# A down projection in seven block products: four groups of feature pairs with sums on the chip, or one group of nine pairs with the inputs' sums made a stage earlier

## The chip, the cores and the metric

The kernel runs on one core of a Trainium2 chip. The engines of a core work side by side, each on its own list of instructions in order: TensorE (PE, matrix products), VectorE (DVE), ScalarE (ACT), GpSimd (POOL) and SyncE (SP, which here issues nearly all DMAs). The metric is the device time of one execution in microseconds (us).

## The reference, cut to what matters

One layer of a hybrid decoder (three kinds of token mixer, then a gated feed-forward part) on 1024 tokens of width 1024. The change lies in the feed-forward part and its last product:

```
fn = rmsnorm(h, ffn_norm_g)
h  = h + (silu(fn @ w_gate) * (fn @ w_up)) @ w_down      # w_gate, w_up: 1024 x 2816, w_down: 2816 x 1024
return rmsnorm(h, final_norm_g)
```

The hidden values `silu(..) * (..)` are 2816 features by 1024 tokens, all in float32.

## The kernel before, in words

**Precision.** Every operand of a product is split into a high part (a rounded copy, ACT, the `act.copy` of `split`) and a low part (operand minus high part, a subtraction on DVE or POOL). A product takes three matmuls: high x high, low x high, high x low.

**Features, pairs, blocks.** The 2816 features are 22 tiles of 128. Two tiles are a pair, so there are 11 pairs (`NP`), p = 0 to 10. Gate and up projection go pair by pair (class `GateUp`, one object a pair, "the gate stage"). A pair's weights and inputs are cut into 2 x 2 blocks, and instead of eight block products seven are made, from sums and differences of blocks (Strassen's scheme in Winograd's form). The products are numbered 1 to 7, and their order in the gate stage is 1, 2, 6, 5, then 7 and 3, then 4. The block outputs of a pair, `out(q, ...)` with q = 0 to 3, are a feature tile and a half of the tokens each; `out` makes sigmoid (ACT) and two multiplications (DVE, L1303 and L1304) into the tile `gs`, and SP stores it to `s_hid` in DRAM (L1305). q = 0 comes after product 2, then q = 3, 1 and 2.

**The down projection** starts when the gate stage ends. It takes the features as pairs too, in 2 x 2 blocks: the left operand is `w_down` (two feature tiles by two output halves, `a11` to `a22`), the right one the hidden values (two feature tiles by two token halves, `b11` to `b22`). Pairs are taken in groups of 2, 2, 2 and 3 (`down_group`). In a group each of the seven products is accumulated in four PSUM banks over the pairs of the group (12 matmuls of 128x512 a pair), in the order 1, 6, 2, 5, 7, 3, 4 on three sets of four banks: A (products 1, 2), B (6, 5, 3), C (7, 4). After product 1 its four banks are copied to `E1` (ACT, L1508) or added to it; after each of the other products DVE adds four banks to the residual in `hF0` to `hF7` (`gather`, L1084). What a product needs is made from whole tiles that SP loaded once (`next_raw`, 512 KB each): sums in place on DVE (`sub` L1081, `add` L1084), and the split of the left and of the right operand, each 128x512, their low parts mostly on POOL (L1078). After the last group `E1` is added to the twelve places that share product 1, on POOL. Features 2304 to 2815 (four tiles) go last, as plain products beside the final norm (`last`, `down`, `last_part`; L1560 to L1562).

**The order.** The source is written product by product, but a scheduler with a model of times of its own lays out each engine's instructions; an engine then runs its list in order, and a wait holds up all that stands behind it.

Of the kernel before, what the change touches and what calls it, by code (L numbers as in the profile page):

```python
# [11 lines left out]
F32 = mybir.dt.float32  # L12
# [20 lines left out]
KV_LORA = 256  # L33
D_FF = 2816
NF = D_FF // 128
EPS = 1e-6
NEG = -1e30

# [20 lines left out]
def tile_hybrid_block(ctx: ExitStack, tc: tile.TileContext, a: dict):  # L59
# [23 lines left out]
    s_hid = dram.tile([NF, 128, SEQ], F32, name="s_hid")  # L83
# [992 lines left out]
    def split(hi, lo, value, eng):  # L1076
        act.copy(hi, value)  # L1077
        eng.tensor_tensor(lo, value, f32(hi), op=ALU.subtract)  # L1078

    def sub(out, x, y):  # L1080
        dve.tensor_tensor(out, x, y, op=ALU.subtract)  # L1081

    def add(out, x, y, eng=None):
        (eng or dve).tensor_tensor(out, x, y, op=ALU.add)  # L1084
# [16 lines left out]
    def q_tile(name):  # L1101
        return tq.tile([128, 512], F32, tag="q", name=name)
# [38 lines left out]
    def operand():  # L1141
        t = hid_tile("op")
        return t[:, HALF[0]], t[:, HALF[1]]
# [92 lines left out]
    class GateUp:  # L1236


        def __init__(self, p):
            self.p = p  # L1240
            self.before = {}
            self.w, self.raw = [], []

        def load_early(self):
# [54 lines left out]
        def out(self, q, gate, up):  # L1299

            h, s = (f1_tile(f1a, "gs", 1), f1_tile(f1a, "sig", 1)) if q == 0 else (q_tile("gs"), q_tile("sig"))
            act.activation(s, gate, AF.Sigmoid)
            dve.tensor_tensor(h, gate, s, op=ALU.mult)  # L1303
            dve.tensor_tensor(h, h, up, op=ALU.mult)  # L1304
# [131 lines left out]
    f2 = ctx.enter_context(tc.tile_pool(name="f2", bufs=1, reuse_waits="tile"))  # L1436
    nraw = nop = 0

    def next_raw(src):
        nonlocal nraw  # L1440
        pl = fr if nraw % 16 < 8 else f2
        nraw += 1
        return raw_tile(pl, src)

    def operand():
        nonlocal nop
        t = fo.tile([128, 1024], F32R, tag="op", bufs=4, name="op") if nop % 16 >= 12 else hid_tile("op")
        nop += 1
        return t[:, HALF[0]], t[:, HALF[1]]
# [5 lines left out]
    LO_DVE = (1, 6, 2)  # L1455

    def down_group(p0, n):
        W, H = [], []
        for e in range(n):
            w, h = ([next_raw(src[2 * (p0 + e) + i]) for i in range(2)] for src in (a["w_down"], s_hid))  # L1460
            W.append((w[0][:, HALF[0]], w[1][:, HALF[0]], w[0][:, HALF[1]], w[1][:, HALF[1]], q_tile("tt")))
            H.append((h[0][:, HALF[0]], h[0][:, HALF[1]], h[1][:, HALF[0]], h[1][:, HALF[1]], q_tile("tt")))

        def operands(i):
            out = []
            for (a11, a12, a21, a22, tw), (b11, b12, b21, b22, th) in zip(W, H):
                if i == 6:
                    sub(a21, a11, a21)
                    sub(b12, b22, b12)
                    sub(tw, a22, a21)  # L1470
                    add(th, b12, b11)
                elif i == 5:
                    add(a11, tw, a11)
                    sub(b11, b22, th)
                elif i == 3:
                    sub(a12, a12, tw)
                elif i == 4:
                    sub(th, b21, th)
                left = {1: a11, 6: tw, 2: a12, 5: a11, 7: a21, 3: a12, 4: a22}[i]
                right = {1: b11, 6: th, 2: b21, 5: b11, 7: b12, 3: b22, 4: th}[i]  # L1480
                if p0 == 0 and i == 1:
                    hl = [wa.tile([128, 1024], F32R, tag=f"w{x}", name=f"w{x}") for x in ("hi", "lo")]
                    pair = [[t[:, s] for t in hl] for s in HALF]
                else:
                    pair = [operand(), operand()]
                split(*pair[0], left, pool)
                split(*pair[1], right, dve if i in LO_DVE else pool)
                out.append(pair)
            return out

        def product(i, banks, start):
            for e, ((wh, wl), (hh, hl)) in enumerate(operands(i)):
                for o in range(4):
                    os = slice(128 * o, 128 * (o + 1))
                    first, last = start and e == 0, e == n - 1
                    pe.matmul(banks[o], wh[:, os], hh, start=first, stop=False, skip_group_check=not start)  # L1496
                    pe.matmul(banks[o], wl[:, os], hh, start=False, stop=False, skip_group_check=not start)  # L1497
                    pe.matmul(banks[o], wh[:, os], hl, start=False, stop=last, skip_group_check=not start)  # L1498

        lo, hi = HALF  # L1500
        A = banks4()
        product(1, A, True)
        if p0 == 0:
            for k in range(KT):
                sp.dma_start(hT[k], s_h[k])
        for o in range(4):
            if p0 == 0:
                act.copy(E1[o], A[o])  # L1508
            else:
                add(E1[o], E1[o], A[o])  # L1510
        B = banks4()
        product(6, B, True)
        gather(B, 4, lo)
        product(2, A, False)
        gather(A, 0, lo)
        product(5, B, False)
        gather(B, 4, hi)
        C = banks4()
        product(7, C, True)
        gather(C, 4, hi)  # L1520
        product(3, B, False)
        gather(B, 0, hi)
        product(4, C, False)
        gather(C, 4, lo)

    p0 = 0
    for n in (2, 2, 2, 3):
        down_group(p0, n)
        p0 += n
# [7 lines left out]
    for e, f in enumerate(range(2 * p0, NF)):  # L1537
        w, h = next_raw(a["w_down"][f]), next_raw(s_hid[f])
        if e < 2:
            hl = [wa.tile([128, 1024], F32R, tag=f"w{x}", name=f"w{x}") for x in ("hi", "lo")]  # L1540
            split(*hl, w, pool)
            W = [[t[:, s] for t in hl] for s in HALF]
        else:
            W = [operand() for _ in HALF]
            for x, s in zip(W, HALF):
                split(*x, w[:, s], pool)
        H = [operand() for _ in HALF]
        for x, s in zip(H, HALF):
            split(*x, h[:, s], dve)
        last.append((W, H))  # L1550

    def down(o, t0, n):
        ts = slice(t0, t0 + n)
# [166 lines left out]
```

## Time and profile before

| | us |
|---|---|
| median of 3 runs (1813.46 to 1816.01) | 1813.62 |
| the profiled execution | 1819.26 |
| its span in the trace | 1817.3 |
| first matmul of the down projection, from the span's start | 1555.0 |
| first matmul of the four plain tiles | 1755.4 |

The times in the trace's rows count from the start of the span. A row of an instruction has its start, its duration, its engine, the source line, and in brackets the idle time of the engine before it and who ended that. A line such as L1084 is that of a helper and is shared by many calls, so the tile's name tells them apart: `hF` with a bank is a gather, `u` and `r` are the gate stage's, `raw` and `tt` are sums of operands.

### The profile page before, as it was taken

The numbers are of one execution on the slowest core, as the hardware profiler recorded it, in microseconds if no ns is written. First come the engines' busy times: TensorE is split into PE (matmuls) and PEld (weight loads), VectorE is DVE, ScalarE is ACT, GpSimd is POOL, SyncE is SP. The second block draws the span as 40 slices with busy tenths as digits, with TensorE's granted clock in tenths as the row PEclk, the third lists the DMA queues.
The fourth block names the chain that finished last, engine by engine and source line by source line (L and its number), as shares of the span: only waits on it lengthen the run. The fifth ranks groups of instructions, "written<-read, shape, count | busy, mean of one in ns | idle before, by whom it ended". The sixth has DMA issues, their size and how long they took to land.

```text
span 1817.3 us, 26447 instructions
## 1 busy us (share of the span) xinstructions
PE 1722.8 (95%) x9769; PEld 1506.0 (83%) x9769; DVE 1214.3 (67%) x1801; ACT 860.0 (47%) x1878; POOL 858.4 (47%) x597
## 2 busy tenths in 40 slices
PE   7969999999999999999999998999999999799997
PEld 7859998999987778998888876778888888677787
DVE  8686655777544673455576558967776667899854
ACT  7545564555566646775544424422232223334333
POOL 4433334343366557563321345634333234678783
PEclk9969999999998999999999998999999999899999
DMA  4211232222443546347221342232222233733102
GB/s 157 60 53 44 78 88 73 64 70 66 116 148 106 187 159 171 103 124 263 78 88 53 108 140 102 64 99 83 80 76 81 71 98 140 286 100 95 47 1 93
DMA packets 121012, 186.93 MB, mean 103 GB/s; under 512 B 21986, under 2 KB 81412, under 8 KB 120884
## 3 DMA queue, kind: packets, MB, share of 16 engines
q1 hardware_dynamic: 101488, 169.69, 29.6%
q10 hardware_dynamic: 19396, 15.56, 2.8%
q8 instruction: 77, 1.26, 0.3%
q14 instruction: 51, 0.42, 0.1%
HBM read 131.61 MB, written 53.60 MB: 102 GB/s over the span
## 4 chain that ended last, share of the span: by engine, by line
PE 68%; DVE 17%; ACT 4%; issue 3%; DMA 3%; POOL 3%; SPq 1%; ACTq 0%; DVEq 0%; POOLq 0%
PE d_ps L142 8%; PE d_ps L143 8%; PE d_ps L144 8%; PE b_ps L1295 7%; PE b_ps L1297 7%; PE b_ps L1296 7%; DVE raw L1081 2%; PE ptg L317 2%; PE b_ps L1498 1%; PE b_ps L1497 1%; PE ptg L319 1%; PE pv L295 1%; PE b_ps L1496 1%; PE pv L296 1%; DVE hF L1084 1%
## 5 line engine op out<-in xcount | busy, mean ns | idle before, releaser
L142 PE MATMUL d_ps<-hnh,whi 128*128 128x384 f32 (+6 forms) x744 | 247.3, 333 | 1.4 <-DVE go L534 0.7
L144 PE MATMUL d_ps<-hnl,whi 128*128 128x384 f32 (+6 forms) x744 | 246.7, 332 | 0.0
L143 PE MATMUL d_ps<-hnh,wlo 128*128 128x384 f32 (+6 forms) x744 | 245.6, 330 | 0.0
L131 POOL TENSOR_TENSOR wlo<-wraw,whi 128x1024 fp32r<-128x1024 f32 (+1 forms) x57 | 135.9, 2385 | 212.0 <-ACT whi L129 203.1
L1078 POOL TENSOR_TENSOR op<-raw,op 128x512 fp32r<-128x512 f32 x83 | 125.2, 1534 | 42.1 <-ACT op L1077 38.9
L142 PEld LDWEIGHTS d_ps<-hnh,whi 128*128 128x128 f32 (+1 forms) x744 | 140.4, 189 | 5.5 <-DVE go L534 1.3
L144 PEld LDWEIGHTS d_ps<-hnl,whi 128*128 128x128 f32 (+1 forms) x744 | 140.6, 189 | 3.3 <-issue 1.0
L143 PEld LDWEIGHTS d_ps<-hnh,wlo 128*128 128x128 f32 (+1 forms) x744 | 140.4, 189 | 2.3 <-issue 0.2
L1295 PE MATMUL b_ps<-T,wh 128*128 128x512 f32 x352 | 138.4, 393 | 0.9 <-DVE u L1084 0.9
L1296 PE MATMUL b_ps<-T,wl 128*128 128x512 f32 x352 | 138.1, 392 | 0.0
L1297 PE MATMUL b_ps<-T,wh 128*128 128x512 f32 x352 | 138.0, 392 | 0.0
L303 DVE TENSOR_TENSOR pl<-ptg,ph 128x512 fp32r<-128x512 f32 (+1 forms) x160 | 99.6, 628 | 46.3 <-ACT ph L302 44.7
L1078 POOL TENSOR_TENSOR wlo<-raw,whi 128x1024 fp32r<-128x1024 f32 (+1 forms) x22 | 52.7, 2395 | 152.9 <-ACT whi L1077 152.9
L669 DVE TENSOR_TENSOR_SCAN cm<-cm,zcol 128x144 f32<-128x144 f32 (+3 forms) x64 | 103.9, 1634 | 17.8 <-ACT cm L667 17.4
L1077 ACT CAST op<-raw 128x512 fp32r<-128x512 f32 x107 | 61.4, 618 | 96.7 <-PE d_ps L1498 49.4
L302 ACT CAST ph<-ptg 128x512 fp32r<-128x512 f32 (+1 forms) x160 | 85.3, 541 | 36.3 <-PE ptg L319 24.7
L1078 POOL TENSOR_TENSOR wl<-raw,wh 128x512 fp32r<-128x512 f32 x46 | 69.8, 1526 | 58.8 <-ACT wh L1077 58.0
L1084 DVE TENSOR_TENSOR hF<-hF,b_ps 128x512 f32<-128x512 f32 (+1 forms) x96 | 59.2, 635 | 46.4 <-PE b_ps L1562 23.9
L486 DVE SCALAR_TENSOR_TENSOR cacc<-d_ps,cw,cacc 128x384 f32<-128x384 f32 (+3 forms) x108 | 61.8, 572 | 38.2 <-ACT cacc L479 36.2
L1077 ACT CAST wh<-raw 128x512 fp32r<-128x512 f32 x88 | 52.9, 616 | 67.0 <-PE b_ps L1297 64.0
L129 ACT CAST whi<-wraw 128x1024 fp32r<-128x1024 f32 (+1 forms) x57 | 58.9, 1033 | 49.4 <-PE d_ps L144 23.4
L1496 PE MATMUL b_ps<-op 128*128 128x512 f32 x183 | 72.8, 401 | 9.9 <-DVE hF L1084 6.2
(452 smaller groups left out, 5352.8 us busy)
## 6 DMA issues: line engine op xcount, KB each, us to landing
raw<-in_w_gate_dram SPq DMA_DIRECT2D x22, 512.0 KB
raw<-in_w_up_dram SPq DMA_DIRECT2D x22, 512.0 KB, 4.1
s_hid<-gs SPq DMA_DIRECT2D x44, 256.0 KB, 2.4
raw<-in_w_down_dram SPq DMA_DIRECT2D x22, 512.0 KB, 5.2
raw<-s_hid SPq DMA_DIRECT2D x22, 512.0 KB, 4.3
wraw<-in_w_o_dram SPq DMA_DIRECT2D x16, 512.0 KB, 4.0
wraw<-in_w_xbc_dram SPq DMA_DIRECT2D x12, 512.0 KB, 3.8
s_xs<-csig SPq DMA_DIRECT2D x24, 192.0 KB, 2.6
```

The source lines that it names most:

```text
L131: pool.tensor_tensor(lo[:, :cols], raw[:, :cols], f32(hi[:, :cols]), op=ALU.subtract)
L142: pe.matmul(ps[:m, :n], wh, mh, start=(kt == 0), stop=False)
L143: pe.matmul(ps[:m, :n], wl, mh, start=False, stop=False)
L144: pe.matmul(ps[:m, :n], wh, ml, start=False, stop=(kt == nkt - 1))
L303: dve.tensor_tensor(pl[:, :n], pt[:, :n], f32(ph[:, :n]), op=ALU.subtract)
L669: dve.tensor_tensor_scan(rev, rev, zcol.to_broadcast([128, n_all]), 1.0, ALU.mult, ALU.add)
L1077: act.copy(hi, value)
L1078: eng.tensor_tensor(lo, value, f32(hi), op=ALU.subtract)
L1295: pe.matmul(banks[j], hi[:, ks], UH[u][k], start=start and k == 0, stop=False, skip_group_check=skip)
L1296: pe.matmul(banks[j], lo[:, ks], UH[u][k], start=False, stop=False, skip_group_check=skip)
L1297: pe.matmul(banks[j], hi[:, ks], UL[u][k], start=False, stop=stop and k == 3, skip_group_check=skip)
L1496: pe.matmul(banks[o], wh[:, os], hh, start=first, stop=False, skip_group_check=not start)
```

## The change

Pairs 2 to 10 become one group of nine, so that each of the seven products runs over nine pairs (108 matmuls) before its banks are read, and each bank is read once where it was read four times. The number of matmuls in the seven products stays 756. Features 0 to 511 (pairs 0 and 1) are the four plain tiles now.

The sums of the hidden values are made in the gate stage, right after the block outputs, with four operations a pair on POOL in the tiles `gs` themselves (`hid_sums`), for p = 2 to 10; SP stores seven tiles of 128x512 a pair to `s_hops`, one for each product, in place of four to `s_hid`.

In the down projection nothing is kept from product to product. For each product and pair SP loads 128x512 pieces (256 KB): the left block or the two or three blocks that its sum is made of, and the right operand from `s_hops`. DVE makes the left sum (one operation in products 7, 5 and 3, two in 6, none in 1, 2 and 4); product 6 stores its left sum to `s_w2`, from which product 3 loads it. Left and right stand side by side in one tile, so that one 128x1024 copy on ACT and one 128x1024 subtraction, now on DVE, split both. The twelve additions of `E1` go to DVE (`pending`). Core of the diff:

```diff
@@ class GateUp, out
-            sp.dma_start(s_hid[2 * self.p + q // 2, :, HALF[q % 2]], h)
+            if self.p < NPLAIN:
+                sp.dma_start(s_hid[2 * self.p + q // 2, :, HALF[q % 2]], h)
+            else:
+                self.h[q] = h
+                self.hid_sums(q)
+        def store(self, i, h):
+            sp.dma_start(s_hops[self.p, i], h)
+        def hid_sums(self, q):
+            h = self.h
+            def into(out, x, y, op):
+                pool.tensor_tensor(out, x, y, op=op)
+            if q in (0, 2, 3):
+                self.store({0: 1, 2: 2, 3: 3}[q], h[q])
+            if q == 1:
+                into(h[1], h[3], h[1], ALU.subtract)
+                self.store(7, h[1])
+                into(h[0], h[1], h[0], ALU.add)
+                self.store(6, h[0])
+                into(h[3], h[3], h[0], ALU.subtract)
+                self.store(5, h[3])
+            if q == 2:
+                into(h[2], h[2], h[0], ALU.subtract)
+                self.store(4, h[2])
@@ down projection (down_group and its four calls are removed)
+    pending = []
+    def operands(i, p):
+        raw = next_raw()
+        left = raw[:, HALF[0]]
+        a11, a21, a12, a22 = (a["w_down"][2 * p + e][:, s] for e in range(2) for s in HALF)
+        ...
+        load(left, {1: a11, 2: a12, 4: a22, 7: a11, 6: a11, 5: a21, 3: a12}[i])
+        if i in (3, 5, 6, 7):
+            more = next_raw()
+            x = load(more[:, HALF[0]], {7: a21, 6: a21, 5: a22, 3: s_w2[p]}[i])
+            if i == 6:
+                y = load(more[:, HALF[1]], a22)
+        load(raw[:, HALF[1]], s_hops[p, i])
+        if i == 5:
+            add(left, left, x)
+        elif i in (3, 6, 7):
+            sub(left, left, x)
+        if i == 6:
+            sub(left, y, left)
+            sp.dma_start(s_w2[p], left)
+        ...
+        split(hi, lo, raw, dve)
+        if pending:
+            pending.pop(0)()
+        return hi, lo
+    def product(i, banks, start):
+        for p in range(NPLAIN, NP):
+            hi, lo = operands(i, p)
+            ...
@@ after product 6 and its gather
     for o in range(4):
         for ot, c in ((o, 1), (o + 4, 0), (o + 4, 1)):
-            add(hT[ot][:, HALF[c]], hT[ot][:, HALF[c]], E1[o], pool)
+            t = hT[ot][:, HALF[c]]
+            pending.append(lambda t=t, e=E1[o]: add(t, t, e))
@@ the four plain tiles
-            for x, s in zip(W, HALF):
-                split(*x, w[:, s], pool)
...
+            hi, lo = operand(), operand()
+            split(hi, lo, raw, dve)
```

How the scheduler laid this out, at three places. First VectorE at a change of products. Before, between the products of the second group, sums (`raw`, `tt`), low parts (`op`) and gathers (`hF` with a bank `b_ps`) alternate:

```order
L1081 TENSOR_TENSOR raw_16133<-raw_16135,tt_16138 128x512
L1078 TENSOR_TENSOR op_16160<-raw_16143,op_16160 128x512
L1084 TENSOR_TENSOR hF4_15788<-hF4_15788,b_ps_16001 128x512
L1081 TENSOR_TENSOR raw_16143<-raw_16145,raw_16143 128x512
L1084 TENSOR_TENSOR raw_16129<-tt_16137,raw_16129 128x512
L1078 TENSOR_TENSOR op_16202<-tt_16138,op_16202 128x512
L1084 TENSOR_TENSOR hF5_15789<-hF5_15789,b_ps_16002 128x512
L1084 TENSOR_TENSOR hF6_15790<-hF6_15790,b_ps_16003 128x512
```

In the changed kernel, where product 1 ends and product 6 begins: `op_16018` is the low part of the last pair of product 1, `grow` and `E1` are the two tiles that hold `E1`, and `raw_16049` is the left operand of the first pair of product 6, whose sum takes the last two rows; its split follows:

```order
L1083 TENSOR_TENSOR op_16018<-raw_16014,op_16017 128x1024
L1089 TENSOR_TENSOR hF0_15849<-hF0_15849,grow_5502 128x512
L1089 TENSOR_TENSOR hF4_15853<-hF4_15853,grow_5502 128x512
L1089 TENSOR_TENSOR hF1_15850<-hF1_15850,grow_5502 128x512
L1089 TENSOR_TENSOR hF5_15854<-hF5_15854,grow_5502 128x512
L1089 TENSOR_TENSOR hF2_15851<-hF2_15851,E1_15857 128x512
L1089 TENSOR_TENSOR hF6_15855<-hF6_15855,E1_15857 128x512
L1089 TENSOR_TENSOR hF3_15852<-hF3_15852,E1_15857 128x512
L1089 TENSOR_TENSOR hF7_15856<-hF7_15856,E1_15857 128x512
L1086 TENSOR_TENSOR raw_16049<-raw_16049,raw_16051 128x512
L1086 TENSOR_TENSOR raw_16049<-raw_16051,raw_16049 128x512
```

Eight of the twelve additions of `E1` have moved ahead of the first sum of product 6; they read what ACT copies from product 1's banks.

Second, SP's queue where the gate stage ends. Before, the residual's eight tiles are loaded behind a store of the gate stage, and whole tiles of the second group follow:

```order
L1305 DMA s_hid_69<-gs_15731 128x512
L1305 DMA s_hid_69<-gs_15763 128x512
L1505 DMA hF0_15784<-s_h_68 128x1024
L1505 DMA hF1_15785<-s_h_68 128x1024
L1505 DMA hF2_15786<-s_h_68 128x1024
L1505 DMA hF3_15787<-s_h_68 128x1024
L1505 DMA hF4_15788<-s_h_68 128x1024
L1505 DMA hF5_15789<-s_h_68 128x1024
L1505 DMA hF6_15790<-s_h_68 128x1024
L1505 DMA hF7_15791<-s_h_68 128x1024
L1131 DMA raw_16129<-in_w_down_dram 128x1024
L1131 DMA raw_16131<-in_w_down_dram 128x1024
```

Now the last of the hidden sums (a store of `gs`, written by POOL) stands ahead, then the last pair of product 1 (`raw_16014`), the residual, and the first piece of product 6's first pair:

```order
L1317 DMA s_hops_69<-gs_15832 128x512
L1498 DMA raw_16014<-in_w_down_dram 128x512
L1498 DMA raw_16014<-s_hops_69 128x512
L1539 DMA hF0_15849<-s_h_68 128x1024
L1539 DMA hF1_15850<-s_h_68 128x1024
L1539 DMA hF2_15851<-s_h_68 128x1024
L1539 DMA hF3_15852<-s_h_68 128x1024
L1539 DMA hF4_15853<-s_h_68 128x1024
L1539 DMA hF5_15854<-s_h_68 128x1024
L1539 DMA hF6_15855<-s_h_68 128x1024
L1539 DMA hF7_15856<-s_h_68 128x1024
L1498 DMA raw_16049<-in_w_down_dram 128x512
```

The loads of product 1's last pair and of product 6's first pair are queued behind that store and behind the residual.

Third, POOL in the gate stage, over one unit of the stage. Before: low parts of weights alone (`s2` for product 6, `wlo` for products 1 and 2, `raw` for product 7):

```order
L1078 TENSOR_TENSOR wl_15514<-s2_15504,wh_15513 128x512
L1078 TENSOR_TENSOR wlo_15501<-raw_15496,whi_15500 128x1024
L1078 TENSOR_TENSOR wl_15518<-s2_15504,wh_15517 128x512
L1078 TENSOR_TENSOR wl_15530<-raw_15489,wh_15529 128x512
L1078 TENSOR_TENSOR wl_15534<-raw_15497,wh_15533 128x512
```

Now the four hidden sums of the pair that has just ended (`gs`) stand among them:

```order
L1083 TENSOR_TENSOR wl_15576<-s2_15562,wh_15575 128x512
L1325 TENSOR_TENSOR gs_15527<-gs_15495,gs_15527 128x512
L1083 TENSOR_TENSOR wl_15588<-raw_15547,wh_15587 128x512
L1325 TENSOR_TENSOR gs_15377<-gs_15527,gs_15377 128x512
L1083 TENSOR_TENSOR wl_15592<-raw_15555,wh_15591 128x512
L1325 TENSOR_TENSOR gs_15495<-gs_15495,gs_15377 128x512
L1325 TENSOR_TENSOR gs_15538<-gs_15538,gs_15377 128x512
L1083 TENSOR_TENSOR wl_15604<-raw_15547,wh_15603 128x512
L1083 TENSOR_TENSOR wl_15608<-raw_15555,wh_15607 128x512
```

Two of the sums have moved ahead of the low parts for product 7 (`wl_15588`, `wl_15592`), all four ahead of those for product 4 (`wl_15604`, `wl_15608`).

More of the change, by code (lines that the diff above doesn't have):

```diff
@@ L35 @@
 NF = D_FF // 128
+NPLAIN = 2
 EPS = 1e-6
@@ L1240, in __init__ @@
             self.p = p
-            self.before = {}
+            self.before, self.h = {}, {}
             self.w, self.raw = [], []
@@ L1454, in tile_hybrid_block @@
     E1 = [t[:, s] for t in (grow, both) for s in HALF]
[L1455 to L1524, printed above, removed]
@@ new lines, in product @@
+    def product(i, banks, start):
+        for p in range(NPLAIN, NP):
+            hi, lo = operands(i, p)
+            hh, hl = hi[:, HALF[1]], lo[:, HALF[1]]
+            for o in range(4):
+                os = slice(128 * o, 128 * (o + 1))
+                first, last = start and p == NPLAIN, p == NP - 1
+                pe.matmul(banks[o], hi[:, os], hh, start=first, stop=False, skip_group_check=not start)
+                pe.matmul(banks[o], lo[:, os], hh, start=False, stop=False, skip_group_check=not start)
+                pe.matmul(banks[o], hi[:, os], hl, start=False, stop=last, skip_group_check=not start)
@@ L1531, in tile_hybrid_block @@
+    lo, hi = HALF
+    A = banks4()
+    product(1, A, True)
+    for k in range(KT):
+        sp.dma_start(hT[k], s_h[k])
+    for o in range(4):
+        act.copy(E1[o], A[o])
+    B = banks4()
+    product(6, B, True)
+    gather(B, 4, lo)
     for o in range(4):
         for ot, c in ((o, 1), (o + 4, 0), (o + 4, 1)):
-            add(hT[ot][:, HALF[c]], hT[ot][:, HALF[c]], E1[o], pool)
-    last = []
[L1537 to L1544, printed above, removed]
-            for x, s in zip(W, HALF):
-                split(*x, w[:, s], pool)
[L1547 to L1550, printed above, removed]
+            t = hT[ot][:, HALF[c]]
+            pending.append(lambda t=t, e=E1[o]: add(t, t, e))
@@ new lines, in tile_hybrid_block @@
+    product(2, A, False)
+    gather(A, 0, lo)
+    product(5, B, False)
+    gather(B, 4, hi)
+    C = banks4()
+    product(7, C, True)
+    gather(C, 4, hi)
+    product(3, B, False)
+    gather(B, 0, hi)
+    product(4, C, False)
+    gather(C, 4, lo)
+    last = []
+    for f in range(2 * NPLAIN):
+        parts = []
+        for src in (a["w_down"][f], s_hid[f]):
+            raw = next_raw()
+            sp.dma_start(raw, src)
+            hi, lo = operand(), operand()
+            split(hi, lo, raw, dve)
+            parts.append([(hi[:, s], lo[:, s]) for s in HALF])
+        last.append(parts)
```

20 lines of the change are left out of this document (12 added, 8 removed).

## The prediction, as written before the changed kernel ran

> **What bounds the kernel now.** I read the page first, then a table of windows for the stages, then TensorE's waits in the down projection, then single instructions.
>
> ```profile
> span 1817.3 us, 26447 instructions
> PE 1722.8 (95%) x9769; PEld 1506.0 (83%) x9769; DVE 1214.3 (67%) x1801; ACT 860.0 (47%) x1878; POOL 858.4 (47%) x597
> ```
>
> TensorE bounds the whole, so only time in which PE waits or runs slowly can be won. The windows below are the down projection, a stretch of the gate stage, and a quiet stretch of the down projection:
>
> ```profile
> core 0: us, PE busy (x) PEld busy (x) DVE busy (x) ACT busy (x) POOL busy (x), PEclk, DMA share, GB/s
> 1555.00:1755.40 200.40, 180.49 (x759) 144.14 (x758) 176.32 (x208) 77.29 (x136) 165.07 (x109) 0.96 0.34 117
> 1200.00:1550.00 350.00, 350.00 (x1514) 283.69 (x1513) 237.78 (x278) 102.93 (x167) 124.72 (x73) 1.00 0.27 88
> 1705.00:1755.00 50.00, 50.00 (x222) 41.41 (x221) 32.55 (x38) 19.41 (x34) 47.29 (x35) 1.00 0.13 43
> ```
>
> The gate stage leaves nothing to win: PE is busy throughout. In the down projection 19.9 of 200.4 us are idle, and DVE (176.32) and POOL (165.07) are nearly as full as PE. PE's waits there, by what ended them:
>
> ```profile
> PE b_ps L1498 <- DVE op L1078: 6.5, 1, 6.5
> PE b_ps L1496 <- DVE hF L1084: 6.2, 5, 1.8
> PE d_ps L1496 <- DVE hF L1084: 3.5, 4, 1.7
> PE b_ps L1496 <- ACT grow L1508: 2.7, 2, 1.5
> PE b_ps L1496 <- DVE u L1084: 1.0, 1, 1.0
> ```
>
> One wait is for a low part, at the start of the stage; 12.4 us are for banks that a gather or the copy to `E1` has not yet emptied; 1.0 us is the gate stage's own. After each wait PE also runs slowly for a while. Its rows at the first wait, at a later one, and in a quiet place:
>
> ```profile
> 1573.35 0.80 PE L1498 MATMUL b_ps<-op 128*128 128x512 f32 x1 [6.49 <-DVE op L1078]
> ...
> 1576.08 0.63 PE L1498 MATMUL d_ps<-op 128*128 128x512 f32 x1
> ...
> 1689.43 0.65 PE L1496 MATMUL b_ps<-op 128*128 128x512 f32 x1 [1.81 <-DVE hF L1084]
> ...
> 1696.51 0.40 PE L1498 MATMUL b_ps<-op 128*128 128x512 f32 x1
> ...
> 1699.70 0.39 PE L1497 MATMUL b_ps<-op 128*128 128x512 f32 x1
> ...
> 1701.97 0.39 PE L1498 MATMUL b_ps<-op 128*128 128x512 f32 x1
> ```
>
> From 1699.70 to 1701.97 ten matmuls start, 0.227 us apart. After the first wait and after the 1.81 us wait (at 1687.62 to 1689.43) the rows stand some 0.43 us apart: 0.63 long instead of 0.39, for about 8 matmuls in the first place and 16 in the second (1689.43 to 1696.51). The seven products have 756 matmuls before and after: 756 x 0.227 = 171.6 us. So 28.8 of the 200.4 us can be won at most: 19.9 of waits, the rest slow clock.
>
> **The change, part by part.** *Gathers.* 72 of 96 bank additions and all twelve E1-into-E1 additions go, and three of four changes of groups. With nine pairs a bank set that has ended lies idle for 108 x 0.227 = 24.5 us at least before it is wanted, and its gather takes at most 12 additions of 0.68 (row below), 8.2 us. So the 12.4 us of waits for banks go, unless VectorE is that late. What is late next is the operand at a change of products, taken up below.
>
> *VectorE and ACT.* The durations:
>
> ```profile
> L791 DVE TENSOR_TENSOR L<-L,cbm x16: 1218/1244/2885, 519.0 to 667.3; 128x1024 f32<-128x1024 f32 x16
> L1084 DVE TENSOR_TENSOR hF<-hF,b_ps 128x512 f32<-128x512 f32 x72 | 47.1, 678 | 20.4 <-PE b_ps L1498 20.3
> L1077 ACT CAST whi<-raw 128x1024 fp32r<-128x1024 f32 x2 | 2.1, 1050 | 5.1 <-DMA raw<-in_w_down_dram 5.1
> L1508 ACT COPY grow<-b_ps 128x512 f32<-128x512 f32 x2 | 1.2, 578 | 0.0
> 1435.23 1.77 DVE L1081 TENSOR_TENSOR raw<-raw,s 128x512 f32<-128x512 f32 x1
> ...
> 1601.14 0.68 DVE L1081 TENSOR_TENSOR raw<-raw 128x512 f32<-128x512 f32 x1
> 1601.74 0.68 DVE L1084 TENSOR_TENSOR tt<-raw 128x512 f32<-128x512 f32 x1
> ```
>
> A subtraction of two SBUF tiles takes 0.68 where POOL is silent (1601.14; the next starts 0.60 later) and 1.77 where POOL works (1435.23, beside the POOL row at 1434.91 below). POOL has next to nothing left in the new stage, so I take 0.68, and 1.24 for a 128x1024 split (the median of L791, the nearest of that size). VectorE then has 63 x 1.24 = 78.1, left sums 45 x 0.68 = 30.6, gathers 24 x 0.68 = 16.3, E1 12 x 0.68 = 8.2, eight splits of the plain tiles 9.9: 143 of some 181 us, 79%. The fullest product is 6: 9 x 1.24 + 18 x 0.68 = 23.4 of 24.5 us. ACT has 71 x 1.05 = 75 us. Neither is the bound, while POOL keeps out; at the long durations both of VectorE's rows would exceed PE, and that is why POOL's place matters.
>
> *The change from product 1 to product 6.* The order puts eight E1 additions ahead of product 6's first sum on VectorE. Product 1 ends at E = 1555.0 + 24.5 = 1579.5. Its banks end one after another, three matmuls apart: the first at E-2.0, its copy (0.58) at E-1.4. Eight additions, 0.60 apart, run to E+3.4, two subtractions to E+4.7, the copy of 128x1024 on ACT (1.05) to E+5.8. PE's first four matmuls there need the high part alone, and cover the split (1.24) but for some tenths. I take a wait of 6.2 us. Bounds: 4 (if the sums overlap the last additions) and 7.1 (E+5.8 and the whole split). No other change of products has additions that must wait for the product just ended ahead of the next operand, so I take 0 there.
>
> *Slow clock.* One wait remains, so one slow stretch: 8 x 0.2 = 1.6 us by the rows at 1573.35, 16 x 0.2 = 3.2 by those at 1689.43; the middle, 2.4. The Trainium skill, on the page "TensorE: Matmul & The Clock Gate", section "Why this matters for your kernels", asks for no idle gaps over about 3 us, since a window of idle halves the clock. Here a gap of 1.81 us was followed by a slow stretch twice as long as the gap of 6.49 was; by the page the 2.4 us fall away once the remaining wait is under 3 us (180.1 in place of 182.5), by the rows they are paid at any such wait.
>
> *Transfers.* Whole tiles of 512 KB, each loaded once, become 171 loads of 256 KB, 44.8 MB; with the residual (4.2 MB), the stores of `s_w2` (2.4) and the plain tiles (4.2) that is 55.6 MB in 181 us, 307 GB/s, where the stage moved 117. The nearest thing is a burst of 256 KB loads on SP:
>
> ```profile
> 840.00:845.00 5.00, 3.00 (x25) 2.76 (x24) 2.44 (x8) 4.32 (x10) 2.85 (x3) 1.00 1.06 391
> 845.00:850.00 5.00, 5.00 (x30) 4.98 (x31) 1.91 (x5) 2.71 (x9) 4.21 (x2) 0.66 1.04 392
> raw<-s_osbh SPq DMA_DIRECT2D x8, 256.0 KB, 5.0
> raw<-s_osbl SPq DMA_DIRECT2D x8, 256.0 KB, 5.2
> 1553.35 3.80 SPq L1505 DMA_DIRECT2D hF<-s_h  x8
> ```
>
> They reached 391 GB/s, so 307 fits with a fifth to spare. An issue takes 3.80 / 8 = 0.47 us on SP: 196 issues are 92 us, half the stage. The tightest place is again the change from 1 to 6: behind the last hidden sum's store SP has 0.5 MB for product 1's last pair, the residual (4.2) and three pieces and a right operand (1.05), 5.8 MB, 14.8 us at 391. That store is not before VectorE's last gate multiplication; I put it at 1563.6, an estimate: some 20 us of work from 1540 (seven splits, five sums, twelve bank additions), then POOL's sum and the issue. The loads land about 1580.4 with 2 us for the way; VectorE wants them at E+3.4 = 1582.9. Margin 2.5 us, cost 0; every us later than that adds one.
>
> *Hidden sums in the gate stage.* Four POOL operations a pair, nine pairs, and three more stores. The rows of one unit:
>
> ```profile
> 1429.22 0.68 DVE L1084 TENSOR_TENSOR u<-r,b_ps 128x512 f32<-128x512 f32 x1
> 1430.22 0.39 PE L1295 MATMUL b_ps<-B,wh 128*128 128x512 f32 x1
> 1434.91 1.54 POOL L1078 TENSOR_TENSOR wl<-s,wh 128x512 fp32r<-128x512 f32 x1 [1.36 <-ACT wh L1077]
> 1441.13 0.68 DVE L1304 TENSOR_TENSOR gs<-gs,r 128x512 f32<-128x512 f32 x1
> 1444.43 1.07 DVE L1304 TENSOR_TENSOR gs<-gs,u 128x512 f32<-128x512 f32 x1
> 1450.05 0.69 DVE L1303 TENSOR_TENSOR gs<-b_ps,sig 128x512 f32<-128x512 f32 x1 [4.55 <-ACT sig L1302]
> ```
>
> A sum on POOL takes about 1.54 (1434.91), four are 6.2 us; POOL is busy 124.72 of 350 us there, 13.8 of a unit of 38.7, so it has room. They can start only behind the multiplications at 1441.13 and 1444.43, and there VectorE idles 4.55 us until 1450.05: I take 0. A gain is excluded, since PE is never idle there. The upper bound: all four lie beside two-tile operations of VectorE, each 1.1 longer (1.77 against 0.68), 4.4 us a unit; PE has 0.3 of slack (bank emptied at 1429.90, written at 1430.22), so 4.1 x 9 = 37 us.
>
> *Edges.* In the last unit VectorE's bank additions for the new product 3 stand behind splits of product 1's pairs. The row of the waits had 1.0 us there; I take 2.0 for this and for what I did not see, between 0 and 4. The last plain-tile split on VectorE, 0.3.
>
> **Sum.** 171.6 + 6.2 + 2.4 + 2.0 + 0.3 = 182.5 us for the stage, against 200.4: 17.9 us less. The profiled execution took 1819.26 (2 beyond its span); 1801.4 becomes its counterpart. The median of the runs is 5.6 lower than that execution, so I take the difference from the median: 1813.62 - 17.9 = 1796 us. No change below 0.2% (3.6 us) can be told from none here.
>
> **The rivals.** *Loads late around the change from 1 to 6.* For it speaks the estimate of 1563.6, with only 2.5 us of margin, and that product 6 takes four loads a pair, 9.4 MB in 24.5 us, 385 GB/s if none were ahead; against it, the loads of four or five of these pairs stand earlier in SP's list, ahead of the residual. Each us beyond the margin is lost: 6 to 13 us, 1802 to 1809.
>
> *The gate stage held up by the hidden sums* (the other side). For it: 1.77 against 0.68 is plain in the rows, and DVE's chain to PE's banks has 0.3 us of slack. Against: the idle 4.55 us. It decides once a unit loses over (17.9 + 3.6) / 9 = 2.4 us, of the 4.1 possible: at 2.5 a unit 1796 + 22.5 = 1818.5, at the bound 1833.
>
> *Transfers bound the stage.* At 260 GB/s, two thirds of the burst, 55.6 MB take 214 us, 31 more than my stage: 1827. Against it speak 391 and 392. The Trainium skill, on "DMA: Bandwidth & Descriptors", section "Rules for kernel authors", wants 1 MiB or more a transfer for full bandwidth; the burst of 256 KB pieces does not bear that out, since many are under way at once.
>
> *Half of the gain goes unseen*, for instance VectorE behind by a us at several changes: within 0.2% of before only if 14 us of the 17.9 are lost.
>
> **Chances and range.** My forecast, 1790 to 1802: 0.68. Late loads, 1802 to 1809: 0.16. Gate stage held up so far that it is slower: 0.08. Transfers: 0.03. Within 0.2%: 0.05. So faster 0.84, same 0.05, slower 0.11. The range is 1790 (wait 4, slow clock 1.6, edges 0: 177.5, 22.9 less) to 1809 (late loads); beyond it lie the cases of loss, 0.16.
>
> **What would show it.** Right: one PE wait of about 6 us at product 6's first matmul, ended by ACT's or VectorE's part of an operand; no wait for `hF`; PE busy 350 of 350 in the gate stage; POOL almost silent in the down projection, VectorE's sums at 0.68 and its splits at 1.24; near 300 GB/s. Wrong: PE waits ended by a DMA in products 1 and 6, PE waits in the gate stage ended by `u` or `r`, splits at 2 us or more.

## The result, and the profile after

| | before | changed |
|---|---|---|
| median of five runs each, us | 1816.01 (1813.46 to 1819.44) | 1797.81 (1793.27 to 1803.84) |
| span of the profiled execution, us | 1817.3 | 1798.2 |
| first matmul of the down projection | 1555.2 | 1555.1 |
| first matmul of the four plain tiles | 1755.3 | 1735.8 |

The changed kernel takes 0.990 of the time before, 95% interval 0.9872 to 0.9929: 18.2 us less between the medians, 19.1 between the profiled spans. All of it lies in the seven products of the down projection, 180.7 us in place of 200.1. (At 1555.0, the time given ahead of the prediction for the kernel before, the weight load of the first matmul starts; the matmul itself starts at 1555.2.) The page of the changed kernel, with the busy time of each engine:

```profile
span 1798.2 us, 26531 instructions
PE 1714.8 (95%) x9769; PEld 1505.1 (84%) x9769; DVE 1159.6 (64%) x1738; ACT 853.9 (47%) x1809; POOL 734.6 (41%) x516
```

The windows: the same stretch of the gate stage, the seven products, one in products 6 and 2, and one late in the stage. In such a row (x) is the number of instructions, PEclk the granted share of TensorE's full clock, and DMA share the mean busy share of the core's DMA engines.

```profile
core 0: us, PE busy (x) PEld busy (x) DVE busy (x) ACT busy (x) POOL busy (x), PEclk, DMA share, GB/s
1200.00:1550.00 350.00, 350.00 (x1513) 283.74 (x1512) 231.73 (x277) 105.93 (x167) 169.51 (x102) 1.00 0.34 114
1555.10:1735.80 180.70, 173.53 (x758) 143.02 (x757) 124.13 (x142) 67.42 (x67) 5.38 (x4) 0.98 0.76 269
1605.00:1630.00 25.00, 25.00 (x112) 20.70 (x111) 23.85 (x29) 11.57 (x13) 0.00 (x0) 1.00 1.05 384
1690.00:1735.00 45.00, 45.00 (x200) 37.26 (x199) 22.97 (x22) 17.59 (x17) 0.00 (x0) 1.00 0.13 36
```

In the gate stage PE is as busy as it was, though POOL has 45 us more in 350. In the seven products POOL has almost nothing (165.07 us before), VectorE 124 us (176), and the transfers run at 269 GB/s, 384 where they are densest. PE's waits from 1540 to 1760 us have shrunk to one line:

```profile
PE b_ps L1531 <- ACT op L1082: 7.2, 1, 7.2
```

It is the wait at product 6's first matmul. What stands around it, on PE, VectorE, ACT and SP's queue (SPq, where a row is the issue of a DMA):

```profile
1579.40 0.39 PE L1533 MATMUL d_ps<-op 128*128 128x512 f32 x1
1586.96 1.65 PE L1531 MATMUL b_ps<-op 128*128 128x512 f32 x3 [7.17 <-ACT op L1082]
...
1578.41 2.83 DVE L1089 TENSOR_TENSOR hF<-hF,grow 128x512 f32<-128x512 f32 x4 [5.49 <-ACT grow L1541]
1581.15 2.58 DVE L1089 TENSOR_TENSOR hF<-hF,E 128x512 f32<-128x512 f32 x4
1584.39 1.44 DVE L1086 TENSOR_TENSOR raw<-raw 128x512 f32<-128x512 f32 x2 [0.65 <-DMA raw<-in_w_down_dram]
...
1585.86 1.04 ACT L1082 CAST op<-raw 128x1024 fp32r<-128x1024 f32 x1 [5.45 <-DVE raw L1086]
...
1565.50 0.32 SPq L1317 DMA_DIRECT2D s_hops<-gs  x1
...
1567.79 4.95 SPq L1539 DMA_DIRECT2D hF<-s_h  x8
1574.04 2.91 SPq L1498 DMA_DIRECT2D raw<-in_w_down_dram  x3
```

Two delays end almost together. VectorE's eight E1 additions run to 1583.7; then it idles 0.65 us for a load. That load is product 6's first pair, issued at 1574.04 behind the residual's eight (1567.79), which stood behind the last hidden sum's store (1565.50). A wait put down to ACT here is ACT waiting for VectorE, and VectorE waiting for SP. Which of the two sets the time, the row alone does not say: the 0.65 us only shows that the load was the later one.

### The profile page after: what moved, and what is told of

Its sections match the earlier page's. It is cut to its first block, busy times and chain, and to the rows that moved or that the text cites. A ratio compares the mean times of both kernels' runs of the same rounds, so it can differ in the third digit from the quotient of the medians.

```text
span 1798.2 us, 26531 instructions
## 1 busy us (share of the span) xinstructions
PE 1714.8 (95%) x9769; PEld 1505.1 (84%) x9769; DVE 1159.6 (64%) x1738; ACT 853.9 (47%) x1809; POOL 734.6 (41%) x516
## 4 chain that ended last, share of the span: by engine, by line
PE 68%; DVE 13%; ACT 5%; DMA 5%; issue 4%; POOL 3%; SPq 1%; ACTq 0%; DVEq 0%; POOLq 0%
PE d_ps L147 8%; PE d_ps L148 8%; PE d_ps L149 8%; PE b_ps L1300 6%; PE b_ps L1302 6%; PE b_ps L1301 6%; PE b_ps L1531 2%; PE b_ps L1533 2%; PE b_ps L1532 2%; PE ptg L322 2%; PE ptg L324 1%; PE pv L301 1%; PE pv L300 1%; DVE cm L674 1%; ACT L L781 1%
## 5 line engine op out<-in xcount | busy, mean ns | idle before, releaser
L1082 ACT CAST op<-raw 128x1024 fp32r<-128x1024 f32 x69 | 71.7, 1050 | 108.9 <-PE d_ps L1533 70.0
L1083 DVE TENSOR_TENSOR op<-raw,op 128x1024 fp32r<-128x1024 f32 x69 | 85.8, 1250 | 45.2 <-ACT op L1082 43.7
L1083 POOL TENSOR_TENSOR wlo<-raw,whi 128x1024 fp32r<-128x1024 f32 x18 | 45.0, 2502 | 107.9 <-ACT whi L1082 107.9
L1089 POOL TENSOR_TENSOR tt<-tt 128x512 f32<-128x512 f32 (+1 forms) x8 | 8.1, 1012 | 193.5 <-ACT tt L1603 193.3
L1086 DVE TENSOR_TENSOR raw<-raw 128x512 f32<-128x512 f32 x58 | 58.8, 1022 | 39.4 <-DMA raw<-in_w_gate_dram 36.1
L1083 POOL TENSOR_TENSOR wl<-raw,wh 128x512 fp32r<-128x512 f32 x46 | 75.0, 1639 | 18.3 <-ACT wh L1082 17.5
```

## The experiments

### Which delay sets the wait at product 6

Only the E1 additions are moved, behind product 6's last split on VectorE (`tc.issue_after(x)` puts what follows behind instruction x in the scheduler's order, `last_on` names an engine's last instruction so far):

```diff
     product(6, B, True)
+    split6 = last_on(DVE)
     gather(B, 4, lo)
...
+            def late(t=t, e=E1[o]):
+                with tc.issue_after(split6):
+                    add(t, t, e)
-            pending.append(lambda t=t, e=E1[o]: add(t, t, e))
+            pending.append(late)
```

> The eight E1 additions stand on VectorE behind product 6's last split instead of ahead of its first sum; the loads keep their order (residual ahead of product 6's first pair). Theory A, the one of the prediction (VectorE's additions are what delays product 6): the 7.2 us wait at product 6's first matmul shrinks to under 1 us and the slow stretch behind it goes, together 8 to 9 us: about 1789 us, ratio to the kernel before about 0.985. Theory B (the pieces for product 6's first pair, queued on SP behind the residual, land at about 1584.4 whatever VectorE does, 0.65 us after its last addition): the wait stays at 6.4 to 7.2 us and the time at 1796 to 1799 us, ratio 0.990.

Measured: 1800.10 us, ratio 0.9896 (0.9878 to 0.9914), the changed kernel's own. The wait is 5.93 us. VectorE now has nothing before product 6's first sum, and its row says what it waits for:

```profile
1583.94 1.42 DVE L1086 TENSOR_TENSOR raw<-raw 128x512 f32<-128x512 f32 x2 [9.97 <-DMA raw<-in_w_down_dram]
```

It idles 9.97 us for the load. Theory A falls: the additions were covered by the loads. The wait is a little under the 6.4 to 7.2 us of theory B, since the load was there at 1583.94 and not 1584.39.

Next the residual's loads go behind product 6's, and what needs the residual (the gather of product 6, the additions) behind a split of product 2:

```diff
-    for k in range(KT):
-        sp.dma_start(hT[k], s_h[k])
...
     product(6, B, True)
-    gather(B, 4, lo)
+    with tc.issue_after(loads6):          # last load of product 6
+        for k in range(KT):
+            sp.dma_start(hT[k], s_h[k])
+    product(2, A, False)
...
+    with tc.issue_after(split2):          # split of product 2's pair 5; the E1 additions too
+        gather(B, 4, lo)
```

> The residual's eight loads stand on SP behind the loads of product 6; the gather of product 6 and all twelve E1 additions stand on VectorE behind the split of product 2's fourth pair. Theory B (queue order on SP): product 6's first pieces are there some 10 us earlier, no wait at its first matmul and no slow stretch: 8 to 9 us less than the changed kernel, about 1789 us, ratio 0.985. Theory A gives the same here, since the additions are away too; only together with the run that moves the additions alone does it tell the two apart. Theory C (the transfers themselves bound the stretch, 386 GB/s over products 6 and 2): the wait comes back later, at an operand of product 6 or 2, and the time is 1794 to 1798 us.

Measured: 1793.83 us, ratio 0.9865 (0.9844 to 0.9887). The wait at product 6 and the slow stretch are gone, and two smaller ones stand in product 2 (its PE rows):

```profile
1620.43 0.96 PE L1537 MATMUL b_ps<-op 128*128 128x512 f32 x3 [1.77 <-ACT op L1082]
...
1622.77 0.50 PE L1538 MATMUL b_ps<-op 128*128 128x512 f32 x1 [1.13 <-DVE op L1083]
```

On VectorE fifteen gathers and additions and one sum stand in a row there, from the first to the split that PE waits for:

```profile
1611.87 1.87 DVE L1089 TENSOR_TENSOR hF<-hF,b_ps 128x512 f32<-128x512 f32 x3
...
1620.29 1.29 DVE L1089 TENSOR_TENSOR hF<-hF,E 128x512 f32<-128x512 f32 x2
1621.49 1.22 DVE L1083 TENSOR_TENSOR op<-raw,op 128x1024 fp32r<-128x1024 f32 x1
```

VectorE has no idle time from 1616 to 1624, so its own list, and not a late load, is what PE waited for there. So the third version spreads them, and moves the residual's loads further back with them: the residual behind product 2's fifth pair, the gather of product 6 behind product 2's eighth split, each E1 addition behind a split of products 5 and 7:

```diff
+    product(2, A, False)
+    with tc.issue_after(loads2):          # load of product 2's pair 6
+        for k in range(KT):
+            sp.dma_start(hT[k], s_h[k])
+    with tc.issue_after(split2):          # split of product 2's pair 9
+        gather(B, 4, lo)
...
         if pending:
-            pending.pop(0)()
+            with tc.issue_after(last_on(DVE)):
+                pending.pop(0)()
```

> The residual's loads now stand on SP behind product 2's fifth pair, the gather of product 6 on VectorE behind product 2's eighth split, and the twelve E1 additions one by one behind splits of products 5 and 7, so that no sixteen operations in a row stand between two splits of product 2, as they did in the run with the residual late (2.9 us of waits there). If that block of sixteen was the cause: no wait over 0.5 us in the seven products, stage of 756 x 0.227 = 171.6 to 173 us from its first matmul to the plain tiles (180.7 in the changed kernel, 175.3 with the residual late), time 1788 to 1792 us, ratio 0.984 to 0.987. If transfers at 386 GB/s are the cause: a wait of 2 to 4 us in product 2 or at product 5's start remains, ended by an operand whose load was late, stage 175 us, 1792 to 1795 us.

Measured: 1788.90 us, ratio 0.9833 (0.9810 to 0.9856), outside the changed kernel's interval: the fastest of all versions here. The window of its seven products has no wait and no slow clock left:

```profile
1554.20:1725.70 171.50, 171.50 (x758) 141.95 (x757) 123.10 (x141) 66.51 (x67) 5.10 (x4) 1.00 0.78 283
```

171.5 us is 756 x 0.227 to a tenth: with 756 matmuls started 0.227 us apart, nothing more is to be had in this stage.

### What carries the gain

The groups of 2, 2, 2 and 3 come back, all else stays:

```diff
+    groups = [(2, 3), (4, 5), (6, 7), (8, 9, 10)]
+    for g in groups:                      # the seven products over the pairs of g
+        ...
+        else:
+            for o in range(4):
+                add(E1[o], E1[o], A[o])
```

> The changed kernel with pairs 2 to 10 in groups of 2, 2, 2 and 3 again: 96 gathers in place of 24, 12 additions into E1, everything else (sums step by step, splits of 128x1024 on VectorE, hidden sums in the gate stage) as changed. If the long group carries the gain: VectorE gets (72 + 12) x 0.68 less the overlap of starts (0.60), 50 to 57 us more, 195 to 200 us of work in a stage of 181, so the stage is bound by VectorE and bank waits return: 1812 to 1820 us, ratio 0.998 to 1.002. If the step-by-step operands and POOL's silence carry it: waits for banks of 2 to 5 us in all and 1800 to 1805 us, ratio 0.991 to 0.994.

Measured: 1807.33 us, ratio 0.9942 (0.9924 to 0.9959), between the two cases. PE's waits in its down projection, and two windows in it:

```profile
PE b_ps L1531 <- ACT op L1082: 11.0, 1, 11.0
PE b_ps L1531 <- DVE hF L1089: 1.9, 2, 1.6
```

```profile
1605.00:1640.00 35.00, 33.33 (x145) 26.67 (x144) 35.00 (x48) 12.87 (x13) 0.00 (x0) 1.00 0.90 309
1640.00:1700.00 60.00, 59.61 (x262) 48.64 (x261) 60.00 (x82) 20.96 (x21) 0.00 (x0) 1.00 0.84 289
```

With 96 gathers again VectorE is full (60.00 of 60), yet PE waits for banks only 1.9 us, not the 12.4 of before. The long wait stands at another place than in the changed kernel: at 1571.4, after 72 matmuls, where products 1, 6 and 2 of the first group have ended and product 5 begins. The gathers of products 6 and 2 stand on VectorE ahead of product 5's first sum, and all but the first wait for their part of the residual, whose loads stand on SP ahead of that sum's pieces; the last gather and the sum:

```profile
1579.18 0.69 DVE L1089 TENSOR_TENSOR hF<-hF,d_ps 128x512 f32<-128x512 f32 x1 [0.57 <-DMA hF<-s_h]
1580.60 0.69 DVE L1089 TENSOR_TENSOR raw<-raw 128x512 f32<-128x512 f32 x1 [0.72 <-DMA raw<-in_w_down_dram]
```

The groups cost 9.5 us between the medians and 8.0 in the stage of the profiled executions. Of these 8.0, 3.8 are the longer wait for the residual and the loads behind it, 11.0 us in place of 7.2, 1.9 are bank waits, and 2.3 lie in the slow stretch and in PE's shorter gaps.

Now POOL gets work back, with the group of nine: the low parts of all right operands. (Before, it made those of all left operands and of the right ones in products 5, 7, 3 and 4.)

```diff
-        split(hi, lo, raw, dve)
+        act.copy(hi, raw)
+        for s, eng in zip(HALF, (dve, pool)):
+            eng.tensor_tensor(lo[:, s], raw[:, s], f32(hi[:, s]), op=ALU.subtract)
```

> The low part of each right operand (63 of 128x512, and the second halves of the plain tiles) goes back to POOL, VectorE keeps the left ones. If VectorE's two-tile operations become long beside POOL (1.77 in place of 0.68, as in the gate stage): POOL is busy 71 x 1.54 = 109 us of 181, VectorE's 45 sums and 71 half splits are long for 60% of the time, 116 x 1.33 = 155 us and 45 us of gathers and additions, 200 us: waits at operands in products 6, 5 and 3, 1803 to 1820 us, ratio 0.993 to 1.002. If the two engines do not hinder each other here, VectorE has 40 us less to do and the time stays at 1796 to 1799 us, ratio 0.990.

Measured: 1806.46 us, ratio 0.9933 (0.9916 to 0.9949). VectorE's groups from 1555 to 1745 us:

```profile
L1520 DVE TENSOR_TENSOR op<-raw,op 128x512 fp32r<-128x512 f32 x55 | 58.5, 1074 | 33.0 <-ACT op L1518 33.0
L1086 DVE TENSOR_TENSOR raw<-raw 128x512 f32<-128x512 f32 x33 | 38.4, 1177 | 0.8 <-DMA raw<-in_w_down_dram 0.7
L1089 DVE TENSOR_TENSOR hF<-hF,b_ps 128x512 f32<-128x512 f32 x18 | 12.0, 678 | 4.2 <-PE b_ps L1534 4.2
```

VectorE has half of each of 63 splits less to do and is busy longer (131.09 against 125.43 us, both from 1555 to 1737): its operations on two SBUF tiles take 1.07 and 1.18 beside POOL, against 0.69 for the same sums in the changed kernel (below). The gathers, which read PSUM, take 0.678 (0.684 in the changed kernel). My 200 us of VectorE were too many, since not all its operations meet POOL, and the waits came in product 6 alone. PE waits 9.5 us at its start, 2.3 more than in the changed kernel: VectorE ended the gate stage 1.8 us later, and the store of the last hidden sum left at 1567.54 in place of 1565.50, with the loads behind it. Three waits in product 6, 3.2 us in all, are for low parts. The other 3 of the 8.5 us that the stage is longer (189.2) lie in slow stretches and short gaps. So the price of POOL's work is measured, but only part of it is the long operations in product 6.

Both undone at once:

> Both undone in the changed kernel: groups of 2, 2, 2 and 3, and the low parts of the right operands on POOL. Apart, the groups cost 8.0 us of stage (188.7 against 180.7) with 1.9 us of bank waits, POOL's low parts 8.5 us. If the bank waits of the kernel before came from the number of gathers alone, the two add up: stage 197, 1815 us, bank waits still near 2 us. If they came from both together, 96 gathers on a VectorE whose two-tile operations POOL makes long (131 us of VectorE work with POOL, plus 84 additions of 0.60 to 0.68, 181 to 188 us), VectorE is the bound in most products: bank waits of 6 to 13 us, as before the change, stage 199 to 206 us, 1817 to 1825 us, ratio 1.000 to 1.004.

Measured: 1816.52 us, ratio 0.9993 (0.9977 to 1.0010): the kernel before, in time. The two parts add up: 9.5 and 8.7 us apart, 18.7 together, and the time is near the 1815 us of the case that adds them. The waits are not those of before, though:

```profile
PE b_ps L1533 <- ACT op L1519: 12.9, 1, 12.9
PE b_ps L1533 <- DVE hF L1089: 3.4, 5, 1.3
PE b_ps L1534 <- DVE op L1521: 3.3, 1, 3.3
PE d_ps L1533 <- DVE hF L1089: 0.2, 1, 0.2
```

16.2 us are for operands and 3.6 for banks, where before it was 6.5 and 12.4. The bank waits lie between the 2 us and the 6 to 13 of the two cases. The time agrees by way of other terms: 12.9 us are the residual and the loads behind it, as in the groups' run. So this run shows that the two parts together are worth the whole gain in the changed kernel, but not why banks were late in the kernel before. That stays open: no run put back the sums of the right operands on the chip, and POOL works 91.8 us in this run's stage, against 164.8 before.

### Three terms that the prediction set at nothing

The hidden sums on VectorE:

```diff
-                pool.tensor_tensor(out, x, y, op=op)
+                dve.tensor_tensor(out, x, y, op=op)
```

> The four hidden sums a pair on VectorE in place of POOL. If the gate stage has room on either engine (the theory of the prediction): VectorE gets 4 x 0.68 = 2.7 us a unit of 38.7 in its idle 4.5 us, PE stays busy 350 of 350 us, 1796 to 1799 us, ratio 0.990. If the sums stand before bank additions that PE waits for (0.3 us of slack): (2.7 - 0.3) x 9 = 22 us more, 1818 us, ratio 1.001.

Measured: 1799.55 us, ratio 0.9892 (0.9871 to 0.9913). The same window of its gate stage:

```profile
1200.00:1550.00 350.00, 350.00 (x1513) 283.74 (x1512) 261.32 (x309) 105.16 (x167) 127.42 (x70) 1.00 0.34 113
```

VectorE takes 30 us more in 350 and PE is none the less busy: the stage has room on either engine.

The E1 additions on POOL, as before the change (`add(t, t, e, pool)`):

> The twelve E1 additions go back to POOL, as before the change. The wait at product 6's first matmul is set by loads (that run with the additions behind product 6 left it at 5.9 us), so taking them from VectorE there gives nothing. If POOL makes VectorE's two-tile operations long in product 6: 12 x 1.5 = 18 us of POOL beside a product that VectorE fills to 95%, about 10 sums and 5 splits at 1.1 us more, 8 to 15 us of VectorE, of which the pairs summed ahead hide some: waits of 3 to 10 us in product 6, 1800 to 1808 us, ratio 0.993 to 0.997. If POOL does not hinder there: 1796 to 1799 us, ratio 0.990.

Measured: 1801.38 us, ratio 0.9907 (0.9887 to 0.9927), not to be told from the changed kernel. PE waits 7.8 us for high parts, 7.0 of it at product 6's start, and 0.3 us for a low part: 1.1 us in product 6 beside the start, less than the 3 to 10 that I expected. So nothing shows that these twelve belong on VectorE.

One piece of 256 KB more a pair in products 5, 7 and 3, which nothing reads:

```diff
             if i == 6:
                 y = load(more[:, HALF[1]], a22)
+            else:
+                load(more[:, HALF[1]], a22)
```

> Products 5, 7 and 3 load one piece of 256 KB more for each pair, which nothing reads: 27 loads, 7.1 MB, 18 us at 386 GB/s. If transfers have the slack of the later products (they end about 38 us ahead of the last of the seven products): no new wait, 1796 to 1800 us, ratio 0.990. If the transfers at 386 GB/s through products 6, 2 and 5 leave no slack: 2.4 MB more in product 5 alone is 6 us of waits, 18 us over the three, 1804 to 1816 us, ratio 0.994 to 1.000.

Measured: 1800.47 us, ratio 0.9892 (0.9866 to 0.9917). A window over products 2, 5, 7 and most of 3, first of this kernel:

```profile
1605.00:1705.00 100.00, 100.00 (x442) 82.77 (x441) 75.73 (x87) 41.09 (x40) 0.00 (x0) 1.00 1.03 382
```

and of the changed kernel:

```profile
1605.00:1705.00 100.00, 100.00 (x443) 82.76 (x442) 75.77 (x88) 40.84 (x40) 0.00 (x0) 1.00 0.88 309
```

Seven MB more are moved in the same 100 us without a wait: the transfers run ahead of PE and have slack after product 6.

## Why the prediction was right, and where its steps were not

*The floor and the sum.* 756 x 0.227 = 171.6 us held to a tenth in the version without waits. The stage was put at 182.5 and took 180.7; the time at 1796 and came out at 1797.8, inside the likeliest case's own range. The gain was put at 17.9 us and is 18.2 between the medians. That it comes so close is in part luck: the edges, 2.0 us too many, and the wait, 1.0 too few, partly cancel.

*The wait from product 1 to 6* was put at 6.2 and measured 7.17, but the step named the wrong cause. It let VectorE's additions set the wait and gave the loads 2.5 us of margin. The additions ended at 1583.7, close to the forecast (1582.9); the loads landed at 1584.4, 4 us after the forecast 1580.4: the last hidden sum's store left at 1565.50 and not 1563.6, and from 1567 to 1585 us the transfers made 353 GB/s and not 391 (the window below). So the rival of the late loads was true in its place, and its price was small only because the additions hid it; with the additions away the wait shrank by 1.2 us and the time by nothing that can be told.

```profile
1567.00:1585.00 18.00, 12.79 (x57) 10.26 (x55) 7.01 (x10) 3.40 (x5) 0.00 (x0) 0.96 0.95 353
```

The late store has a cause that the prediction had no term for. VectorE's last multiplication ended at 1560.50, near the 1560 assumed, but POOL's last hidden sum started only at 1564.19. It is made in place, in the tile whose old content SP was just storing as product 2's operand, and its row waits for that store:

```profile
1559.82 0.68 DVE L1309 TENSOR_TENSOR gs<-gs,u 128x512 f32<-128x512 f32 x1
1564.19 1.28 POOL L1325 TENSOR_TENSOR gs<-gs 128x512 f32<-128x512 f32 x1 [4.84 <-DMA s_hops<-gs]
```

A tile of its own for this sum might bring the store, and the loads behind it, up to 3.7 us forward; no run tried it. That the additions alone would have held PE nearly as long is read from their end at 1583.7; no run had the loads early and the additions in place.

*Gathers.* That the waits for banks go was right: none is left. The reason given, 24.5 us between the end of a bank set and its next use, does not account for most of them: with four groups and the same 96 gathers, but POOL silent, 1.9 us of the 12.4 came back, and 3.6 with the low parts of the right operands on POOL as well. What made the rest is not shown.

*VectorE.* The durations held. The groups of the changed kernel from 1586 to 1736 us:

```profile
L1083 DVE TENSOR_TENSOR op<-raw,op 128x1024 fp32r<-128x1024 f32 x61 | 74.2, 1224 | 34.4 <-ACT op L1082 32.9 <-DMA raw<-s_hops 1.5
L1086 DVE TENSOR_TENSOR raw<-raw 128x512 f32<-128x512 f32 x28 | 18.8, 686 | 0.4 <-DMA raw<-in_w_down_dram 0.3
```

1.224 and 0.686, against the 1.24 and 0.68 taken. VectorE's total in the stage, 124 us, is under the 143 forecast: operations that follow each other at once overlap by up to 0.08 us, and part of product 1's and the plain tiles' work falls outside the window.

*Slow clock.* "After each wait PE also runs slowly for a while" was wrong, and the rows before showed it: behind a wait of 1.70 us in the kernel before, the matmuls after the first start 0.23 apart.

```profile
1613.88 0.50 PE L1496 MATMUL d_ps<-op 128*128 128x512 f32 x1 [1.70 <-DVE hF L1084]
1614.21 0.39 PE L1497 MATMUL d_ps<-op 128*128 128x512 f32 x1
1614.44 0.40 PE L1498 MATMUL d_ps<-op 128*128 128x512 f32 x1
```

There were only two slow stretches beside thirteen waits. The granted clock in them (PEclk):

```profile
1566.80:1577.00 10.20, 3.71 (x10) 2.91 (x10) 8.91 (x8) 2.31 (x5) 5.95 (x4) 0.50 1.04 365
1689.70:1696.40 6.70, 5.96 (x14) 4.18 (x14) 6.70 (x10) 1.14 (x2) 2.47 (x3) 0.50 0.00 0
```

The first began as the wait of 6.49 us did, right behind waits of 1.49 and 1.17 us, so most of it passed while PE was idle and only 8 slow matmuls followed; the second began at the end of the wait of 1.81 us and ran through 14 matmuls, not 16, with the wait of 0.74 among them. At 0.2 us a matmul they cost some 1.6 and 2.8 us. Of the 8.9 us that the prediction called slow clock, about 2 are the pipeline: a wait is counted from a matmul's end (0.39 after its start), while in a stream the next starts after 0.227, so each of thirteen costs 0.16 more than its idle time. About 1.5 are the longer first matmul (0.50). The term for the changed kernel, 2.4, measured 180.7 - 171.6 - 7.2 = 1.9 all the same, since its one wait was of the long kind.

*Hidden sums and edges.* Zero was right for the gate stage: PE 350.00 of 350, on POOL and on VectorE alike. The 2.0 us for the last unit did not come; with the wait and the slow stretch taken off, nothing is left over.

*Transfers.* 256 KB pieces ran at 384 GB/s through products 6 and 2, as the burst had shown, and 7 MB more cost nothing. So the rival of too slow transfers is refuted, and that of the gate stage by PE's 350.00 of 350 there.

## What to carry to other kernels

Where two delays end within a microsecond of each other, taking one away can show the other and win nothing, as it did with the additions here: ask of each what would be late without it, and move both. Loads that are wanted late, as the residual is, belong in a queue behind those wanted first, and the work that needs them goes behind in small pieces, since sixteen operations in a row between two operands were a wait of their own. Keeping a second engine out of a stage can be worth more than the work it takes over: POOL's half splits cost 8.7 us here.

## What the runs showed of the hardware

VectorE's operations on two SBUF tiles of 128x512 took 1.07 and 1.18 us on average beside a POOL that was at work for 100.7 of 182 us, 0.69 without it, and the gathers, with one operand in PSUM, 0.678 and 0.684. The Trainium skill, on the page "SBUF — State Buffer", section "Who interferes with whom", says that two SBUF inputs contend with GpSimd's reads and that one does not; these rows agree.

In the down projection, the slow stretch of TensorE came with each wait of 5.9 us and more, behind 3.33 us (both parts undone), behind 2.05 us (POOL's low parts; rows 0.63 long after it) and behind 1.81 us, and not behind a single one of 1.77 us (the version with the residual late) or less. In the kernel before, the clock had already fallen when its wait of 6.49 us began, behind two of 1.49 and 1.17 us; whether short waits close together add up, no run tested. The Trainium skill, "TensorE: Matmul & The Clock Gate", section "Why this matters for your kernels", puts the limit near 3 us: nearer to these rows than the prediction's "each wait", but above the waits of 1.81 and 2.05 us that a stretch followed.

With one piece more a pair, loads of 256 KB from SP's queue kept 382 GB/s over 100 us, at a DMA share of 1.03; a load there landed 5.4 us after its issue (median), in which time 382 GB/s move 2.1 MB, so some eight were under way at once, as an estimate from these figures. The Trainium skill's "DMA: Bandwidth & Descriptors", section "Rules for kernel authors", asks for 1 MiB or more a transfer for full bandwidth; no run here has such loads beside these to compare.
